# Input loads in another order, retention pair sums on VectorE, and output-projection operands ahead of their gates

## The chip, the cores and the metric

The kernel runs on one core of a Trainium2 chip, as one launch. The metric is device time in microseconds (us) of that launch; the median over several executions counts.

The engines are named as the profile names them: PE is TensorE (matrix products and transposes; PEld are its weight loads), DVE is VectorE, ACT is ScalarE, POOL is GpSimd, and SP is SyncE, which here issues most of the transfers. Each engine works through its own list of instructions in order, and semaphores tie the lists together.

## The reference, cut to what matters

A trunk of two layers over 1024 rows of 1024 features. Each layer scales and shifts its input by vectors made from the conditioning vector `c`, runs a mixer, adds and normalizes, and runs a convolutional feed-forward part.

```python
e = jax.nn.silu(c @ cond_w + cond_b)
for i in range(DEPTH):                       # layer 0: gated_deltanet, layer 1: retention
    mod = (e @ ada_w[i] + ada_b[i])[:, None, :]
    sh1, sc1, g1, sh2, sc2, g2 = jnp.split(mod, 6, axis=-1)
    y = mixers[i % N_MIXERS](x * (1.0 + sc1) + sh1)
    x = layer_norm(DN_ALPHA * x + (1.0 + g1) * y, ln_g[i, 0], ln_b[i, 0])
    y = conv_ffn(x * (1.0 + sc2) + sh2, ...)
    x = layer_norm(DN_ALPHA * x + (1.0 + g2) * y, ln_g[i, 1], ln_b[i, 1])

# retention (4 heads, 8 chunks of 128 rows), its scan and its end
o = einsum(q_n, state) * xi ;  state = state * gamma_c + einsum(k_n * zeta, v_n)
o = intra + inter
o = _standardize(o, 1e-6)                    # per row and head
return (o * silu(gate)) @ w_out
```

## The kernel before

Rows are held transposed for the matrix products. Products are done in three passes: an operand is split into a high part (made by ACT, L89) and the rest (made by DVE, L90), and high x low, low x high and high x high are summed in a PSUM tile (`acc`, `sc` and `mm` are the three kinds of tile). The text is written roughly in order of the work, and a scheduler of the build then decides from it how each engine's list stands; so an edit at one place can also swap neighbours elsewhere.

**The start.** The 1024 rows are two halves of 512, and `x` is loaded half by half and by columns: `load_x(half, c)` issues four transfers for columns `c`. `mod_loads(g)` loads the weight columns of group g (two feature tiles) for the scale `sc1` and shift `sh1`; `mod_cols(g)` multiplies them by `e` on DVE (eight instructions, L500 and L502), sums over partitions by eight small matrix products on PE (L507, result in an `mm` tile), and adds the biases on DVE (L509, L514). `turn` transposes `x` on PE (L521) into an `mm` tile, and `hold` copies transposed tiles aside by ACT (L532), so that they wait for their scale. `first_k(half, f)` scales feature tile f (ACT, L538), splits it and runs the first projections' products on it: into `acc` tiles for half 0, into `sc` tiles for half 1 (L110 to L112). Beside this, steps of later layers' modulation (`bg_ada`, L221 and L223 on DVE) run in the background; each loads two 128x512 tiles (L213) and frees their places when DVE has read them.

**The retention core.** `core(h)` runs eight chunk steps n of head h. `ret_back(h, n, po)` ends each: row statistics on DVE (L1818 to L1821), one power on POOL (L1822, `mv`), the standardized row `on` (DVE, L1824), and after a pause (`yield RL["b"]`) the load of its gate rows, four transposes, and the product with the gate (`ot`, DVE, L1833). The output projection uses a Strassen scheme of seven products over blocks 11, 12, 21, 22 of its operands, and so needs sums of blocks. For n < 4 the blocks 11 and 12 are stored in DRAM (`od`). For n > 3 those of the same columns are loaded again (`op`, L1851), block 22 is stored by ACT's queue (L1852), and four pair sums S1, S2, S4, S3 are made by POOL (L1855), in place, each stored by SP (L1856). The fourth, S3, overwrites the tile from which block 22 is stored. While the core runs, PE also works on the projections of the values (`ret_v`) and on the first products of the output projection.

**The output projection** (`proj_gen`, with `gate` in retention): step n of 56 is one of seven products and one of eight operand blocks j; `ops(n)` loads and splits its two operands (`ab`, `bb`). `ops_ahead(n)` does this a step before it is used. In retention, products 0 and 1 wait with `gate(j)` until head j//2 has stored its blocks (event `("ob", h)`).

Of the kernel before, what the change touches and what calls it, by code (L numbers as in the profile page):

```python
# [15 lines left out]
P = 128  # L16
# [3 lines left out]
HALF = 512  # L20
# [6 lines left out]
ABLK = ("11", "12", "22", "S1", "S2", "S3", "S4")  # L27
# [6 lines left out]
def trunk_kernel(ctx: ExitStack, tc, A):  # L34
    nc = tc.nc
    pe, act, dve, pool, sp = nc.tensor, nc.scalar, nc.vector, nc.gpsimd, nc.sync
# [9 lines left out]
    def tl(tag, shape, dt=F32, name=None):  # L46
        return sb.tile(shape, dt, tag=tag, name=name or tag, bufs=BUFS[tag])
# [13 lines left out]
    def mm_tile():  # L61
        return ps.tile([P, HALF], F32, tag="mm", name="mm", bufs=2)

    def sc_tile():
        return ps.tile([P, HALF], F32, tag="sc", name="sc", bufs=2)
# [16 lines left out]
    def hs(half):  # L82
        return slice(half * HALF, (half + 1) * HALF)
# [71 lines left out]
    def by_cols(banks, w, v, k):  # L155
        for j, bank in enumerate(banks):
            pe.matmul(bank[:, 0:1], w[:, j * P:(j + 1) * P], v[:, k:k + 1], start=(k == 0), stop=(k == KT - 1))
# [33 lines left out]
    def bias_cols(i, j):  # L191
        return ada_b[:, i * 48 + j * 8:i * 48 + j * 8 + 8]
# [294 lines left out]
    def mod_loads(g):  # L487
        w = mw[g] = [tl("hTb" if g < 2 else "qkv", [P, HALF] if g > 1 else [P, 2, HALF], name="mvw") for _ in range(4 if g < 2 else 8)]
        for j, t in enumerate(w):
            sp.dma_start(t, A["ada0"][g][:, 2 * j:2 * j + 2] if g < 2 else A["ada0"][g][:, j])  # L490

    def mod_cols(g):
        w = mw[g]
        n = 2 * P if g == 0 else HALF
        a = tl("t2", [P, HALF], name="mva")[:, 0:n]
        bank = [sc_tile(), sc_tile()] if g == 0 else None
        for k in range(KT):
            wk = w[k // 2][:, k % 2] if g < 2 else w[k]
            if k == 0:
                dve.tensor_scalar(a, wk[:, 0:n], e[:, 0:1], None, ALU.mult)  # L500
            else:
                dve.scalar_tensor_tensor(a, wk[:, 0:n], e[:, k:k + 1], a, ALU.mult, ALU.add)  # L502
            if g == 0:
                by_cols(bank, wk[:, n:], e, k)
        pt = mm_tile()
        for j in range(n // P):
            pe.matmul(pt[:, j:j + 1], a[:, j * P:(j + 1) * P], ones[:, 0:1], start=True, stop=True)  # L507
        c = slice(2 * g, 2 * g + 2)
        dve.scalar_tensor_tensor(sc1[:, c], pt[:, 0:2], 1.0, bias_cols(0, 1)[:, c], ALU.add, ALU.add)  # L509
        if g == 0:  # L510
            for j in range(2):
                dve.tensor_add(sh1[:, j:j + 1], bank[j][:, 0:1], bias_cols(0, 0)[:, j:j + 1])
        else:
            dve.tensor_add(sh1[:, c], pt[:, 2:4], bias_cols(0, 0)[:, c])  # L514
# [3 lines left out]
    def turn(half, f):  # L518
        pt = mm_tile()
        for t in range(4):  # L520
            pe.transpose(pt[:, t * P:(t + 1) * P], xt[half][t][f // 4][:, f % 4 * P:(f % 4 + 1) * P], ident)  # L521
        return pt

    def hold(half, fs):
        for f in fs:
            if half == 0 and f > 3:
                if f % 2 == 0:
                    xT["w"] = tl("wr", [P, 2, HALF], name="xT")
                t = xT["w"][:, f % 2]
            else:  # L530
                t = tl("auh" if half else "xT", [P, HALF], name="xT")
            act.activation(t, turn(half, f), AF.Copy)  # L532
            xT[half, f] = t

    def first_k(half, f):
        src = xT[half, f] if (half, f) in xT else turn(half, f)
        tmp = tl("t2", [P, HALF])
        act.activation(tmp, src, AF.Identity, bias=sh1[:, f:f + 1], scale=sc1[:, f:f + 1])  # L538
        ht = two(("hTa", "hTb")[half], F32R, "hT")
        split(ht[0], ht[1], tmp)  # L540
        hT[half].append(ht)
        if accs[half] is None:
            accs[half] = [sc_tile(), sc_tile()] if half else acc4()
        for n, acc in enumerate(accs[half]):
            mm3(acc, ws[n], f, ht, f == 0, f == KT - 1)
# [4 lines left out]
    def load_x(half, c):  # L550
        for t in range(4):
            if half:
                xt[1][t][c] = tl("auh", [P, HALF], name="xt")
            r0 = half * HALF + t * P
            sp.dma_start(xt[half][t][c], xin[r0:r0 + P, hs(c)])
# [12 lines left out]
    mod_cols(1)  # L568
    hold(0, range(4, 8))
    mod_loads(2)  # L570
    load_x(1, 0)
    first_k(0, 2)
    first_k(0, 3)
    mod_cols(2)
    hold(1, range(4))
    mod_loads(3)
    load_x(1, 1)
    first_k(0, 4)
    first_k(0, 5)
    mod_cols(3)  # L580
    for f in range(4):
        first_k(1, f)
    first_k(0, 6)
# [35 lines left out]
    events = {}  # L619
# [18 lines left out]
    def emit(name, lat=0.0):  # L638
        events[name] = clk[0] + lat
# [635 lines left out]
    def proj_gen(nj, ablk, wsrc, slots, xsrc, G, final, ln_next, tag, ltags, dst, key, mm=pe.matmul, gate=None, gain=None):  # L1275
# [48 lines left out]
        def ops(n):  # L1324
            if n in ready:
                return ready.pop(n)
            p, j = n // nj, n % nj
            an, bn = prods[p][:2]
            early = not gate and p < (7 if final else 5)
            ra, rb = ablk(an, j), bblk(bn, j)  # L1330
            last = an == "22"
            at = ltags[0] if last and j >= nj - ltags[3] else ("wl", "hTb", "wr")[n % 3] if early else ("wl", "wr")[n % 2]
            wt = (ltags[1] if last and j >= nj - ltags[2] else ("wh", "hTb", "hTb")[n % 3] if early
                  else ("wh", "auh")[n % 2] if gate and p > 1 else "wh")
            a = two(at, F32R, "ab")
            split(a[0], a[1], ra)
            w = two(wt, F32R, "bb")
            split(w[0], w[1], rb)
            if bn == "22":
                dve.tensor_tensor(X[j], rb, X[j], ALU.subtract)  # L1340
            with after("a"):
                for st in steps[n + ahead:n + ahead + 1]:
                    load_b(*st)
            return a, w

        def ops_ahead(n):
            if n < len(steps) and not (gate and n <= 2 * nj):
                ready[n] = ops(n)

        xts = [[], []]  # L1350
# [108 lines left out]
        steps = [(bn, j) for _, bn, _ in prods for j in range(nj)]  # L1459
# [4 lines left out]
        for p, (an, bn, fin) in enumerate(prods):  # L1464
# [8 lines left out]
            for j in range(nj):  # L1473
# [4 lines left out]
                a, w = ops(p * nj + j)  # L1478
# [178 lines left out]
    od = dr.tile([8, 7, P, HALF], F32, tag="od", name="od")  # L1657
# [58 lines left out]
    for t in range(4):  # L1716
        if t % 2 == 0:
            xw = tl("lane", [P, 2, HALF], name="xlo")
        x = xw[:, t % 2]
# [96 lines left out]
    def ret_back(h, n, po):  # L1816
        st = tl("st", [P, 2, 6], name="rst")
        dve.bn_stats(st[:, 0], po)  # L1818
        mv = tl("s8", [P, 4], name="mv")
        dve.bn_aggr(mv[:, 0:2], st[:, 0])  # L1820
        dve.tensor_scalar(mv[:, 2:3], mv[:, 1:2], 1e-6, None, ALU.add)  # L1821
        pool.tensor_tensor(mv[:, 3:4], mv[:, 2:3], mhalf[:, 0:1], ALU.pow)  # L1822
        on = tl("t2", [P, HALF], name="on")
        dve.tensor_scalar(on, po, mv[:, 0:1], mv[:, 3:4], ALU.subtract, ALU.mult)  # L1824
        yield RL["b"]
        sl = slice(n * P, (n + 1) * P)
        g = tl("cv", [P, 516], name="gt")[:, 0:HALF]
        sp.dma_start(v4(g), gd[4 * h:4 * h + 4, :, sl].rearrange("j p t -> p j t"))
        pt = mm_tile()
        for j in range(4):  # L1830
            ptr(pt[:, j * P:(j + 1) * P], on[:, j * P:(j + 1) * P])
        ot = tl("cv", [P, 516], name="ot")[:, 0:HALF]
        dve.tensor_mul(ot, pt, g)  # L1833
        s4 = slice(n % 4 * P, (n % 4 + 1) * P)

        def pair_view(t):
            return t.rearrange("p (j a f) -> p a j f", a=2, f=P)

        def blk(nm):
            return od[2 * h:2 * h + 2, ABLK.index(nm), :, s4].rearrange("j p t -> p j t")  # L1840

        ov = pair_view(ot)
        if n < 4:
            for a, nm in enumerate(("11", "12")):
                anchor["x", 1] = act.dma_start(blk(nm), ov[:, a])
            if n == 3:
                emit(("ob", h), RL["o"])
            return
        pv = pair_view(tl("cv", [P, 516], name="op")[:, 0:HALF])
        for a, nm in enumerate(("11", "12")):  # L1850
            sp.dma_start(pv[:, a], blk(nm))  # L1851
        act.dma_start(blk("22"), ov[:, 1])  # L1852
        for d, x, y, op, nm in ((ov[:, 0], ov[:, 0], ov[:, 1], ALU.add, "S1"), (pv[:, 0], ov[:, 0], pv[:, 0], ALU.subtract, "S2"),
                                (pv[:, 1], pv[:, 1], pv[:, 0], ALU.subtract, "S4"), (ov[:, 1], ov[:, 1], pv[:, 0], ALU.subtract, "S3")):
            pool.tensor_tensor(d, x, y, op)  # L1855
            sp.dma_start(blk(nm), d)  # L1856

    def load_qk(h, j):
# [134 lines left out]
```

## Time and profile before

| | us |
|---|---|
| median of 3 runs | 2937.2 (2934.97 to 2941.72) |
| the profiled execution's own time | 2931.49 |
| its span in the trace | 2929.3 |
| busy in the span: PE | 2808.1 (96%) |
| DVE | 2198.4 (75%) |
| ACT | 1316.2 (45%) |
| POOL | 421.1 (14%) |
| retention core and first products of its output projection (1780 to 2140): PE busy | 346.83 of 360.00 |

Times within a trace count from the start of the span. A row of the timeline gives the start, the duration, the engine, the line, the operation with its output and inputs, and in brackets how long the engine was idle before it and what released it. A row of the waits gives an instruction, what it waited for, the total, the number of times and the longest. The mean granted clock of PE was 0.989 of full speed in this execution.

### The profile page before, as it was taken

To read this page: it belongs to the slowest core of one execution; us is meant where nothing else is said; L and a number is where in the kernel's file an instruction comes from. 1 tells how busy PE (TensorE), PEld (TensorE's weight loads), DVE (VectorE), ACT (ScalarE), POOL (GpSimd) and SP (SyncE) were. 2 spreads that over 40 slices of the span, in tenths; PEclk is the share of its full clock that TensorE was granted. 3 is DMA by queue.
4 is the path that set the end of the run, shared out by engine and by line. 5 is a ranking of instruction groups with operands and counts; after the bars stand their busy time and mean duration, and the time that the engine had idled before them with its cause. 6 is when DMAs were issued, how large, how long until landed. Compare 5 with 4: busy or idle time off the path is not lost. (4 is left out here: it accounts for less than half of the span.)

```text
span 2929.3 us, 38823 instructions
## 1 busy us (share of the span) xinstructions
PE 2808.1 (96%) x13638; PEld 2296.3 (78%) x13638; DVE 2198.4 (75%) x3965; ACT 1316.2 (45%) x2457; POOL 421.1 (14%) x485
## 2 busy tenths in 40 slices
PE   8998999999999999999999999999999899999997
PEld 7777877887778888887787877777778688888786
DVE  6695687556788888897687766666697887778888
ACT  3755465443544444536443332221345544444443
POOL 0311220134011111100000000223201011111001
PEclk9999999999999999999999999999999999999999
DMA  8122221354344444863434454555564233335753
GB/s 309 64 80 80 98 91 44 105 187 148 108 150 159 163 157 147 316 218 123 157 110 173 149 181 149 165 172 163 189 235 155 94 137 108 108 108 202 262 158 119
DMA packets 239234, 442.35 MB, mean 151 GB/s; under 512 B 22848, under 2 KB 76352, under 8 KB 239040
## 3 DMA queue, kind: packets, MB, share of 16 engines
q1 hardware_dynamic: 206832, 387.96, 39.4%
q10 hardware_dynamic: 29760, 43.00, 4.0%
q0 software_dynamic: 2448, 8.91, 0.8%
q8 instruction: 107, 1.75, 0.2%
q14 instruction: 87, 0.71, 0.1%
HBM read 331.26 MB, written 108.53 MB: 150 GB/s over the span
## 5 line engine op out<-in xcount | busy, mean ns | idle before, releaser
L1466 PE MATMUL acc<-bb,ab 128*128 128x512 f32 x1800 | 427.5, 393 | 6.5 <-DVE pa L1441 2.5
L1466 PEld LDWEIGHTS acc<-bb,ab 128*128 128x128 f32 x1800 | 338.0, 189 | 81.4 <-DVE bb L90 3.8
L630 PE MATMUL acc<-hT,wh 128*128 128x512 f32 x960 | 300.3, 394 | 0.0
L1605 POOL TENSOR_TENSOR o<-o 128x512 f32<-128x512 f32 x88 | 121.1, 1387 | 810.6 <-DVE o L1598 680.4
L89 ACT ACTIVATE ab<-ar 128x512 fp32r<-128x512 f32 x210 | 129.0, 624 | 184.2 <-PE acc L1466 93.3
L1159 PE MATMUL acc<-T,wb 128*128 128x512 f32 x840 | 204.2, 392 | 7.2 <-DVE wb L90 7.2
L630 PEld LDWEIGHTS acc<-hT,wh 128*128 128x128 f32 x960 | 183.0, 191 | 34.0
L630 PE MATMUL acc<-hT,wl 128*128 128x512 f32 x480 | 202.8, 422 | 0.8 <-DVE qkv L993 0.5
L1159 PEld LDWEIGHTS acc<-T,wb 128*128 128x128 f32 x840 | 157.9, 189 | 43.7 <-DVE wb L90 11.1
L90 DVE TENSOR_TENSOR ab<-ar,ab 128x512 fp32r<-128x512 f32 x210 | 146.4, 703 | 44.2 <-ACT ab L89 44.2
L90 DVE TENSOR_TENSOR wb<-mm,wb 128x512 fp32r<-128x512 f32 x216 | 145.2, 684 | 23.4 <-ACT wb L89 21.7
L90 DVE TENSOR_TENSOR wb<-wr,wb 128x512 fp32r<-128x512 f32 x162 | 111.3, 688 | 65.7 <-ACT wb L89 63.8
L1225 ACT ACTIVATE pc<-acc 128x512 f32<-128x512 f32 x143 | 84.7, 592 | 160.5 <-PE acc L1159 91.6
L89 ACT ACTIVATE wh<-wr 128x1024 fp32r<-128x1024 f32 x101 | 107.0, 1061 | 110.2 <-PE acc L630 50.3
L89 ACT ACTIVATE wb<-mm 128x512 fp32r<-128x512 f32 x216 | 122.3, 593 | 72.8 <-DVE mm L1205 72.1
L90 DVE TENSOR_TENSOR wl<-wr,wh 128x1024 fp32r<-128x1024 f32 x85 | 105.5, 1241 | 61.2 <-ACT wh L89 59.1
L89 ACT ACTIVATE wb<-wr 128x512 fp32r<-128x512 f32 x162 | 99.7, 627 | 96.5 <-DMA wr<-in_ffn_up 53.0
L449 DVE SCALAR_TENSOR_TENSOR qkv<-raw,vc,qkv 128x512 f32<-128x512 f32 x144 | 112.3, 783 | 34.8 <-ACT qkv L447 30.7
L630 PE MATMUL acc<-wh,hT 128*128 128x512 f32 x384 | 135.5, 415 | 0.7 <-DVE vv L90 0.7
L1584 DVE SCALAR_TENSOR_TENSOR o<-g,vc,o 128x512 f32<-128x512 f32 (+2 forms) x176 | 135.2, 786 | 0.7
L223 DVE SCALAR_TENSOR_TENSOR ada<-mvw,e,ada 128x512 f32<-128x512 f32 x140 | 105.9, 757 | 27.0 <-DMA mvw<-in_ada_w 26.5
L110 PE MATMUL acc<-T,wb 128*128 128x512 f32 x292 | 116.6, 399 | 9.9 <-DVE wb L90 9.4
(626 smaller groups left out, 6876.5 us busy)
## 6 DMA issues: line engine op xcount, KB each, us to landing
wr<-in_ffn_up SPq DMA_DIRECT2D x96, 512.0 KB, 4.3
ad<-o SPq DMA_DIRECT2D x154, 256.0 KB, 2.2
ar<-ad SPq DMA_DIRECT2D x154, 256.0 KB, 4.2
mvw<-in_ada_w SPq DMA_DIRECT2D x48, 512.0 KB, 5.5
Br<-in_ffn_down SPq DMA_DIRECT2D x66, 256.0 KB, 3.3
mvw<-in_ada_w SPq DMA_DIRECT2D x64, 256.0 KB, 3.0
wr<-in_ret_wv SPq DMA_DIRECT2D x32, 512.0 KB, 4.2
ar<-od SPq DMA_DIRECT2D x56, 256.0 KB, 5.0
```

Of the source, the lines that this page charges most:

```text
L89: act.activation(dst_h, src, AF.Copy)
L90: eng.tensor_tensor(dst_l, src, dst_h, ALU.subtract)
L110: mm(acc, wl[:, k], hl[0], start=first, stop=False)
L223: dve.scalar_tensor_tensor(a, wr[kk], e[:, k:k + 1], a, ALU.mult, ALU.add)
L449: dve.scalar_tensor_tensor(oh, raw[:, 3 - j:515 - j], w[:, 3 - j:4 - j], oh, ALU.mult, ALU.add)
L630: pq(pe.matmul(out, lhsT, rhs, start=start, stop=stop, **kw), cost)
L1159: return pe.matmul(*a, skip_group_check=True, **kw)
L1225: act.activation(t, X, AF.Copy)
L1466: mm_ = (lambda *a, p=p, onto=onto, **kw: (mm if p < 2 else pe.matmul)(*a, skip_group_check=onto, **kw))
L1584: dve.scalar_tensor_tensor(tv, gv[:, c0 - j:c1 - j], w[:, 2 - j:3 - j], tv, ALU.mult, ALU.add)
L1605: pool.tensor_tensor(o[d], o[x], o[y], op)
```

## The change

It has three parts. At the start, the loads of group 3's weight columns (`mod_loads(3)`) stand right behind those of group 2, ahead of the load of half 1's first columns, and `hold(1, range(4))` and the load of half 1's second columns (`load_x(1, 1)`) stand behind `mod_cols(3)`. In the output projection, the operands of a step are made a step ahead in products 0 and 1 too, if the block's event has been emitted, and always from step 16 on. In the retention core the reload of blocks 11 and 12 is issued ahead of the pause, and the four pair sums are VectorE's.

```diff
@@ -568,16 +568,16 @@
     mod_loads(2)
+    mod_loads(3)
     load_x(1, 0)
     first_k(0, 2)
     first_k(0, 3)
     mod_cols(2)
-    hold(1, range(4))
-    mod_loads(3)
-    load_x(1, 1)
     first_k(0, 4)
     first_k(0, 5)
     mod_cols(3)
+    hold(1, range(4))
+    load_x(1, 1)
     for f in range(4):
         first_k(1, f)
@@ -1344,7 +1344,9 @@
         def ops_ahead(n):
-            if n < len(steps) and not (gate and n <= 2 * nj):
+            if gate and n < 2 * nj and ("ob", n % nj // 2) not in events:
+                return
+            if n < len(steps):
                 ready[n] = ops(n)
@@ -1822,6 +1824,18 @@
         dve.tensor_scalar(on, po, mv[:, 0:1], mv[:, 3:4], ALU.subtract, ALU.mult)
...
+        if n > 3:
+            pv = pair_view(tl("cv", [P, 516], name="op")[:, 0:HALF])
+            for a, nm in enumerate(("11", "12")):
+                sp.dma_start(pv[:, a], blk(nm))
         yield RL["b"]
@@ -1846,13 +1852,10 @@
-        pv = pair_view(tl("cv", [P, 516], name="op")[:, 0:HALF])
-        for a, nm in enumerate(("11", "12")):
-            sp.dma_start(pv[:, a], blk(nm))
         act.dma_start(blk("22"), ov[:, 1])
         for d, x, y, op, nm in (...):
-            pool.tensor_tensor(d, x, y, op)
+            dve.tensor_tensor(d, x, y, op)
             sp.dma_start(blk(nm), d)
```

The numbers of instructions stay the same but for the sums: DVE has 64 more, POOL 64 fewer. Lines behind the new code shift: `on` is L1826 afterwards, the sums are L1858.

PE's list at the start, from the last products that group 2 allows to the small matrix products of group 3 (L507): before, transposes and products of half 1 (`sc`) stand on both sides of it.

```order
L112 MATMUL sc<-hT,wh 128x512
L110 MATMUL sc<-hT,wl 128x512 x2
L507 MATMUL mm<-ones,mva 128x1 x4
L521 MATMUL mm<-cst,xt 128x128 x4
L111 MATMUL sc<-hT,wh 128x512
L112 MATMUL sc<-hT,wh 128x512
L111 MATMUL sc<-hT,wh 128x512
```

The same place of the list afterwards:

```order
L111 MATMUL acc<-hT,wh 128x512
L112 MATMUL acc<-hT,wh 128x512
L507 MATMUL mm<-ones,mva 128x1 x4
L521 MATMUL mm<-cst,xt 128x128 x18
L110 MATMUL sc<-hT,wl 128x512 x2
L521 MATMUL mm<-cst,xt 128x128 x2
L111 MATMUL sc<-hT,wh 128x512
```

All products of half 1 now stand behind the small products of group 3 and behind 18 transposes; 16 of these are `hold(1, range(4))`, and the last two read columns that `load_x(1, 1)` brings.

SP's list of transfers at the same place, before (L490 is `mod_loads`, L555 `load_x`, L213 the background step):

```order
L490 DMA mvw<-in_ada 128x512 x8
L555 DMA xt<-in_x 128x512 x4
L490 DMA mvw<-in_ada 128x512 x8
L213 DMA mvw<-in_ada_w 128x512 x2
L102 DMA wr<-in_gdn_wqkv 128x1024
L213 DMA mvw<-in_ada_w 128x512 x2
L555 DMA xt<-in_x 128x512 x4
L213 DMA mvw<-in_ada_w 128x512 x6
```

And afterwards:

```order
L490 DMA mvw<-in_ada 128x512 x16
L555 DMA xt<-in_x 128x512 x4
L213 DMA mvw<-in_ada_w 128x512 x2
L102 DMA wr<-in_gdn_wqkv 128x1024
L213 DMA mvw<-in_ada_w 128x512 x8
L555 DMA xt<-in_x 128x512 x4
```

The second `L555 x4` is `load_x(1, 1)`; ten background loads stand ahead of it now, and four did. On DVE, the end of group 3 (the last L502, then L509 and L514) among the background steps, before:

```order
L502 SCALAR_TENSOR_TENSOR mva<-mvw,e,mva 128x512
L223 SCALAR_TENSOR_TENSOR ada<-mvw,e,ada 128x512
L90 TENSOR_TENSOR hT<-t_563,hT 128x512
L223 SCALAR_TENSOR_TENSOR ada<-mvw,e,ada 128x512
L90 TENSOR_TENSOR hT<-t_574,hT 128x512
L223 SCALAR_TENSOR_TENSOR ada<-mvw,e,ada 128x512
L509 SCALAR_TENSOR_TENSOR v_172<-mm,vc 128x2
L514 TENSOR_TENSOR v_173<-mm,vc 128x2
L223 SCALAR_TENSOR_TENSOR ada<-mvw,e,ada 128x512
```

And afterwards:

```order
L502 SCALAR_TENSOR_TENSOR mva<-mvw,e,mva 128x512
L223 SCALAR_TENSOR_TENSOR ada<-mvw,e,ada 128x512
L502 SCALAR_TENSOR_TENSOR mva<-mvw,e,mva 128x512
L223 SCALAR_TENSOR_TENSOR ada<-mvw,e,ada 128x512 x2
L509 SCALAR_TENSOR_TENSOR v_172<-mm,vc 128x2
L514 TENSOR_TENSOR v_173<-mm,vc 128x2
L223 SCALAR_TENSOR_TENSOR ada<-mvw,e,ada 128x512
```

One more background step moved ahead of the last L502; two still stand between it and L509, one behind L514. In the retention core, DVE's list at step n = 5 of a head, before, from the mask product `sT` to the split of the next values (`vv`):

```order
L1763 TENSOR_TENSOR sT<-mm,dx 128x128
L1833 TENSOR_TENSOR ot<-mm,gt 128x512
L90 TENSOR_TENSOR sThl<-sT,sThl 128x128
L1818 BN_STATS rst<-sc 128x6
L1820 BN_AGGR mv<-rst 128x2
L1821 TENSOR_SCALAR mv<-mv 128x1
L1824 TENSOR_SCALAR on<-sc,mv 128x512
L90 TENSOR_TENSOR vv<-acc,vv 128x512 x2
```

And afterwards:

```order
L1765 TENSOR_TENSOR sT<-mm,dx 128x128
L1847 TENSOR_TENSOR ot<-mm,gt 128x512
L90 TENSOR_TENSOR sThl<-sT,sThl 128x128
L1858 TENSOR_TENSOR ot<-ot 128x2x128
L1858 TENSOR_TENSOR op<-ot,op 128x2x128
L1858 TENSOR_TENSOR op<-op 128x2x128
L1820 BN_STATS rst<-sc 128x6
L1822 BN_AGGR mv<-rst 128x2
L1823 TENSOR_SCALAR mv<-mv 128x1
L1826 TENSOR_SCALAR on<-sc,mv 128x512
L1858 TENSOR_TENSOR ot<-ot,op 128x2x128
L90 TENSOR_TENSOR vv<-acc,vv 128x512 x2
```

S1, S2 and S4 stand ahead of the statistics, and S3 (`ot<-ot,op`) between `on` and the split of the values. On DVE at the end of product 1 of the output projection (`c` is its four results) and the start of product 2, before:

```order
L90 TENSOR_TENSOR bb<-Br,bb 128x512 x2
L1425 TENSOR_TENSOR c<-acc,rowb 128x512 x4
L1313 TENSOR_TENSOR Br<-Bw 128x512 x2
L90 TENSOR_TENSOR bb<-Br,bb 128x512
L1313 TENSOR_TENSOR Br<-Bw 128x512
L90 TENSOR_TENSOR ab<-ar,ab 128x512
```

And afterwards:

```order
L90 TENSOR_TENSOR bb<-Br,bb 128x512
L1427 TENSOR_TENSOR c<-acc,rowb 128x512 x4
L90 TENSOR_TENSOR bb<-Br,bb 128x512
L1313 TENSOR_TENSOR Br<-Bw 128x512 x2
L90 TENSOR_TENSOR ab<-ar,ab 128x512
```

The operand `ab` of step 16 stands one instruction nearer to the four results, still behind them.

More of the change, by code (lines that the diff above doesn't have):

```diff
@@ L1824, in ret_back, with blk, pair_view @@
         dve.tensor_scalar(on, po, mv[:, 0:1], mv[:, 3:4], ALU.subtract, ALU.mult)
+        s4 = slice(n % 4 * P, (n % 4 + 1) * P)
+        def blk(nm):
+            return od[2 * h:2 * h + 2, ABLK.index(nm), :, s4].rearrange("j p t -> p j t")
+        def pair_view(t):
+            return t.rearrange("p (j a f) -> p a j f", a=2, f=P)
+        if n > 3:
+            pv = pair_view(tl("cv", [P, 516], name="op")[:, 0:HALF])
+            for a, nm in enumerate(("11", "12")):
+                sp.dma_start(pv[:, a], blk(nm))
         yield RL["b"]
@@ L1833, in ret_back @@
         dve.tensor_mul(ot, pt, g)
[L1834 to L1840, printed above, removed]
         ov = pair_view(ot)
```

## The prediction

> **What bounds the kernel now.** I read the page first: how much of the span each engine works.
>
> ```profile
> span 2929.3 us, 38823 instructions
> PE 2808.1 (96%) x13638; PEld 2296.3 (78%) x13638; DVE 2198.4 (75%) x3965; ACT 1316.2 (45%) x2457; POOL 421.1 (14%) x485
> ```
>
> PE is idle for 121.2 us in all (2929.3 - 2808.1). The change does not alter PE's products, so it can only move that idle time and the clock at which PE runs. I therefore read, in each of the three places, what PE waits for, and walk the new lists with durations of the old rows. At the start the view of PE in order of time shows this:
>
> ```profile
> 53.74 1.18 PE L521 MATMUL mm<-cst,xt 128*128 128x128 f32 x8
> 56.29 1.97 PE L521 MATMUL mm<-cst,xt 128*128 128x128 f32 x8 [1.37 <-ACT xT L532]
> 57.91 1.94 PE L110 MATMUL acc<-hT,wl 128*128 128x512 f32 x4
> ...
> 64.27 0.62 PE L110 MATMUL sc<-hT,wl 128*128 128x512 f32 x2
> ...
> 67.44 0.95 PE L507 MATMUL mm<-ones,mva 128*128 128x1 f32 x8
> 68.25 0.64 PE L521 MATMUL mm<-cst,xt 128*128 128x128 f32 x4
> ...
> 84.17 0.73 PE L110 MATMUL sc<-hT,wl 128*128 128x512 f32 x2 [1.09 <-ACT hT L89]
> 86.00 0.50 PE L111 MATMUL sc<-hT,wh 128*128 128x512 f32 x1 [1.09 <-DVE hT L90]
> ...
> 87.42 1.12 PE L633 MATMUL mm<-cst,ab 128*128 128x128 f32 x4
> ```
>
> Between 57.91 and 67.44 PE never waits: behind the 24 products of half 0 (to 64.27) it has products of half 1 to do while DVE makes group 3's columns. The clock in the same stretch (columns: window, its length, PE busy, granted clock):
>
> ```profile
> 54.00:56.30 2.30, 0.93 (x9) 0.97 0.03 7
> 56.30:58.00 1.70, 1.70 (x9) 0.50 0.74 154
> 58.00:60.00 2.00, 2.00 (x8) 0.60 0.97 349
> 60.00:64.00 4.00, 4.00 (x19) 1.00 0.94 340
> 84.00:88.00 4.00, 2.65 (x9) 0.86 0.00 0
> 88.00:92.00 4.00, 4.00 (x15) 0.71 0.18 55
> ```
>
> After an idle stretch of 1.4 us PE ran at half clock for some 3.3 us, a loss of about 1.7 us; the two stalls at 84 and 86 were followed by a loss of 4 x 0.14 + 4 x 0.29 = 1.7 us too.
>
> **The start, step by step.** Rows of ACT, DVE and SP's queue in order of time (the last row is of the page: transfers of this size, and the median time to landing):
>
> ```profile
> 54.23 1.52 ACT L538 ACTIVATE t<-xT,v,v 128x512 f32<-128x512 f32 x2 [5.48 <-DVE v L514]
> ...
> 60.80 10.31 SPq L213 DMA_DIRECT2D mvw<-in_ada_w  x6
> ...
> 64.23 0.74 DVE L502 SCALAR_TENSOR_TENSOR mva<-mvw,e,mva 128x512 f32<-128x512 f32 x1
> 64.98 0.75 DVE L223 SCALAR_TENSOR_TENSOR ada<-mvw,e,ada 128x512 f32<-128x512 f32 x1
> ...
> 68.63 0.75 DVE L223 SCALAR_TENSOR_TENSOR ada<-mvw,e,ada 128x512 f32<-128x512 f32 x1 [1.04 <-DMA mvw<-in_ada_w]
> ...
> mvw<-in_ada_w SPq DMA_DIRECT2D x64, 256.0 KB, 3.0
> ```
>
> 1. Without the 16 transposes of `hold(1, ...)`, PE goes from group 2's small products (done 53.7) to half 0's products. These need ACT's scaling (done 55.75 for both tiles) and a split, 0.6: 56.3. Idle 2.6, of which 1.37 were there before.
> 2. The 24 products, at half clock to about 59.7 and then at 0.23 us each as in the rows 57.91 to 64.27: done about 63.4.
> 3. Then L507 of group 3. Its last input is the last L502, which ended at 64.97. Two splits moved from ahead of it to behind (1.3), but a background step moved ahead, whose operand, issued at 60.80, lands 2.8 later at best (63.6); 63.65 + 0.67 + 0.74 is 65.1 again. PE idle 63.4 to 65.1: 1.7. The small products take 0.8, four transposes 0.5: 66.4.
> 4. The next transposes need the tile that L509 and L514 release. These stand behind two background steps (L223). The second's load can be issued when the step ahead has freed its place. In the rows above, from the end of L223 at 65.73 to the next use of its place at 68.63 are 2.9 us. Before the last L502 the freeing step now ends at about 64.4; + 2.9 = 67.3, + 0.75 + 0.15: 68.2. PE idle 1.8.
> 5. Twelve transposes at 0.11 to 0.15: 69.9. The 17th reads `load_x(1, 1)`. On SP this stands behind ten background loads, the last of which needs the place that the step behind L514 frees, at about 69.8. With the median 3.0 to landing: 73.2. PE idle 3.3.
> 6. From there PE has its products without a wait up to the end of the stretch, where the last tile's scaling and split leave about 1.5 (before: 1.09 + 1.09).
>
> Idle afterwards 2.6 + 1.7 + 1.8 + 3.3 + 1.5 = 10.9; before, 1.37 + 1.09 + 1.09 = 3.6. That is 7.3 more. The clock goes down once more (behind 63 to 73, up to 1.7) and may stay up at 84 to 92 (1.7): I take zero. **Term +7, from +4 to +9**: the low end with landings 1 us sooner in steps 4 and 5 and no new half-clock stretch, the high end with that stretch. I let all of it reach the end: PE's share of the span is 96%, and no idle stretch near the start is long enough to take it up.
>
> [...]
>
> **The pair sums.** The waits of PE, and one of DVE's, from 1780 to 2140 (total, times, longest):
>
> ```profile
> PE sc L1466 <- DVE ab L90: 4.1, 1, 4.1
> PE sc L630 <- DVE on L1824: 4.0, 4, 1.8
> PE acc L630 <- DVE ab L90: 2.8, 1, 2.8
> PE mm L633 <- DVE on L1824: 1.5, 3, 1.2
> PE sc L630 <- DVE Sr L1798: 0.6, 1, 0.6
> PE acc L630 <- DVE bb L90: 0.2, 1, 0.2
> ...
> DVE on L1824 <- POOL mv L1822: 28.1, 24, 3.4
> ```
>
> PE waits 13.2 us in 360. 6.1 of these (`on`, `Sr`) hang on the retention steps, and DVE's `on` waits 28.1 us for the power on POOL, which often stands behind pair sums. So at best 6.1 go. What the 64 sums cost on DVE has no row of their form; the nearest, with DVE's share:
>
> ```profile
> L1763 DVE TENSOR_TENSOR sT<-mm,dx 128x128 f32<-128x128 f32 x32 | 9.0, 281 | 0.0
> L1761 DVE SCALAR_TENSOR_TENSOR kz<-mm,vc,kz 128x256 fp32r<-128x256 f32 x28 | 13.4, 478 | 13.5 <-ACT kz L1760 13.5
> 1780.00:2140.00 360.00, 229.76 (x426) 1.00 0.55 174
> ```
>
> Between 281 (128x128) and 478 (128x256, another operation) I take 0.42 us: 64 x 0.42 = 27 us (18 to 31). DVE has 130 us free there, which covers them, and most stand where DVE waited for POOL. Without that cover they would all be late for `on`, and 27 us would be on the path of the steps.
>
> The new wait is another one. S3 overwrites the tile from which ACT's queue stores block 22, and must wait for that store; on POOL this held up POOL alone:
>
> ```profile
> 1845.84 0.39 ACTq L1852 DMA_DIRECT2D od<-ot  x1
> 1850.76 0.81 DVE L1824 TENSOR_SCALAR on<-sc,mv 128x512 f32<-128x512 f32 x1 [2.35 <-POOL mv L1822]
> 1853.23 0.73 POOL L1855 TENSOR_TENSOR ot<-ot,op 128x256 f32<-128x256 f32 x1 [2.51 <-DMA od<-ot]
> ...
> 1857.15 0.63 PE L633 MATMUL mm<-cst,on 128*128 128x128 f32 x4 [0.17 <-DVE on L1824]
> ```
>
> These are rows of ACT's queue, DVE, POOL and PE. The store took 7.4 us (1845.84 to 1853.23). On DVE, S3 stands at step 5 behind `on` and ahead of two splits of values (0.64 each) and the next statistics. DVE would stand until 1853.2 with these queued; the two splits that were done by 1852.8 come after, and the next `on`, for which PE already waited at 1857.15, is about 1.4 us later. Steps 4 are alike with S3 ahead of the statistics. With 8 steps 4 and 5 in four heads at up to 0.8 on average, the upper end is +6; the lower is -6.1. Most of the other stores land well inside the pause, and only some of `on`'s waits are behind a sum: **term +1, from -6 to +6**, the middle with the one place that I can place on its upper side.
>
> [...]
>
> The earlier reload (SP) moves two issues, about 0.4 us each, ahead of the gate rows' load; SP is not waited for there, so I cost it at nothing; its cover is the pause, and without it `ot` would be 0.9 us later.
>
> **Operands ahead.** The view of time, DVE, at the 4.1 us wait:
>
> ```profile
> 2130.39 1.28 DVE L1313 TENSOR_TENSOR Br<-Bw 128x512 f32<-128x512 f32 x2
> 2131.85 0.69 DVE L90 TENSOR_TENSOR bb<-Br,bb 128x512 fp32r<-128x512 f32 x1 [0.17 <-ACT bb L89]
> 2132.46 0.68 DVE L1313 TENSOR_TENSOR Br<-Bw 128x512 f32<-128x512 f32 x1
> 2133.06 0.69 DVE L90 TENSOR_TENSOR ab<-ar,ab 128x512 fp32r<-128x512 f32 x1
> ```
>
> Behind product 1's results (2130.4) `ab` of step 16 was the fifth instruction and is now the fourth: `bb`, two `Br`, `ab`, each 0.60 to 0.69 behind the one ahead, end at about 2133.0, against 2133.7. **Term -0.7, from -4 to 0**; all 4.1 would go only if it stood ahead of the results, which it does not. The 2.8 us wait is step 0's, which isn't made ahead.
>
> **Sum.** +7 + 1 - 0.7 = +7.3 on the profiled 2931.5, so 2938.8. That execution lies 5.7 us below the median of the three runs; against the median 2937.2 the forecast is 2944.5. 0.2% is 5.9 us, about what a measurement of this kernel tells from no change.
>
> **Rivals.**
> - *The start does not open.* If L507 of group 3 can run by 63.4 because its columns are done 1.7 us sooner, L514 and the background steps move up with it, and `load_x(1, 1)` lands under half 1's first products. For it: group 3's loads are issued earlier. Against: at 64.23 its DVE step waited for nothing that is a load of its own. Start 0: +0.3, 2937.5, the same. Chance 0.17.
> - *Faster: DVE is freed of POOL.* Place: 1857 to 2134. If `on` comes 28.1/24 = 1.2 us sooner in nearly each step, DVE is ahead everywhere, and all of PE's 13.2 us of waits there go: 7 - 13.2 = -6.2, 2931. It decides as soon as the core gives back over 12.9 (7 + 5.9). Against: 6.9 of the 13.2 are operand waits behind PE's own results. Chance 0.12.
> - *Slower still: the store blocks DVE.* With stores of 7 us in most steps 4 and 5: core +6, sum +12.3, 2949.5. For it: 7.4 us in the row above, with 174 GB/s moved beside it. Against: on POOL the wait was 2.5 us. Chance 0.13.
> - *No net change:* the swaps that the scheduler makes elsewhere (each under 1 us) and the ends of the ranges cancel. 2937 to 2940. Chance 0.05.
>
> **How the numbers follow.** The forecast itself has 0.53, its own range +3 to +11 (2940 to 2948). Slower by over 0.2% (above 2943.1): 0.43 of the forecast, all of the blocked store, nothing else: 0.56. The same: 0.10 of the forecast, 0.14 of the unopened start, 0.04 of the faster case, 0.05 of the last: 0.33. Faster: 0.08 of its case and 0.03 of the unopened start: 0.11. The range 2930 to 2951 holds the faster case's price and the blocked store's, and leaves out 0.2.
>
> **What would show it.** In the changed profile: PE idle before L507 of group 3, before its transposes, and before the 17th, in sum near 6.8, and the L633 row near 94.5 where 87.42 stood; DVE's wait of `on` for POOL down from 28.1 to below 10, and in its place waits of L1858 for `od<-ot` of some 10 us in all; sums near 0.42 us; PE's wait at 2133.80 near 3.4. The prediction is wrong if L633 stands before 90, or if PE's waits for `on` vanish without new ones.

## The result and the profile after

| | before | after |
|---|---|---|
| median of 8 runs, us | 2938.4 (2934.1 to 2941.7) | 2945.5 (2942.0 to 2948.1) |
| ratio | | 1.0022 (95%: 1.0013 to 1.0032), +6.5 us |
| span of the profiled execution | 2929.3 | 2944.2 |

The change makes the kernel slower by 0.22%. The two profiled executions lie 14.9 us apart, more than the medians do: that of before lies 7 us below its median, that of after at its own. The page of after begins:

```profile
span 2944.2 us, 38789 instructions
PE 2817.0 (96%) x13638; PEld 2300.2 (78%) x13638; DVE 2220.9 (75%) x4029; ACT 1315.8 (45%) x2457; POOL 372.9 (13%) x421
```

PE's idle time went from 121.2 to 127.2 us. Its busy time rose by 8.9 us although it runs the same 13638 products: the mean granted clock is 0.986 here and was 0.989. Both parts must be followed. Counted by the number of the PE instruction, the 14.9 us split into 9.9 up to the 600th, 2.3 on to the 8800th (the retention core's first step), -1.4 to the 10280th (the start of product 2), 4.6 to the 13200th (in the last product) and -0.4 to the end. Of the 4.6 us, 2.8 are idle time of PE; no run here takes that stretch apart. PE in order of time at the start, after:

```profile
52.47 0.95 PE L507 MATMUL mm<-ones,mva 128*128 128x1 f32 x8
55.87 2.07 PE L110 MATMUL acc<-hT,wl 128*128 128x512 f32 x4 [2.45 <-ACT hT L89]
...
65.30 1.26 PE L507 MATMUL mm<-ones,mva 128*128 128x1 f32 x8 [2.20 <-DVE mva L502]
66.42 1.09 PE L521 MATMUL mm<-cst,xt 128*128 128x128 f32 x4
68.40 2.89 PE L521 MATMUL mm<-cst,xt 128*128 128x128 f32 x12 [0.89 <-DVE v L514]
74.16 0.66 PE L521 MATMUL mm<-cst,xt 128*128 128x128 f32 x2 [2.86 <-DMA xt<-in_x]
76.15 0.69 PE L521 MATMUL mm<-cst,xt 128*128 128x128 f32 x2 [0.48 <-DMA xt<-in_x]
...
95.75 0.51 PE L111 MATMUL sc<-hT,wh 128*128 128x512 f32 x1 [0.71 <-DVE hT L90]
97.18 0.66 PE L633 MATMUL mm<-cst,ab 128*128 128x128 f32 x4 [0.22 <-ACT ab L595]
```

The brackets sum to 9.8 us; before, those of this stretch came to 3.7 (1.37, 0.16, 1.09, 1.09). L633 stands 9.8 us later than the 87.42 of before; counted from the small products of group 2 (52.47 here, 52.93 before) it is 10.2. The clock (window, length, PE busy, granted clock):

```profile
64.00:68.00 4.00, 2.21 (x12) 0.74 0.45 149
68.00:72.00 4.00, 2.89 (x12) 0.50 0.50 154
72.00:78.00 6.00, 3.37 (x10) 0.50 0.54 175
78.00:84.00 6.00, 6.00 (x27) 0.87 0.25 89
...
88.00:92.00 4.00, 4.00 (x19) 1.00 0.00 0
```

PE stands idle for 28% to 45% of each of the first three windows, and from about 66 on it runs at half clock, and on for 1.6 us when the work is back. Busy time x (1 - clock) in these four rows is 4.5 us; the half clock of before at 84 to 92 (1.5) is gone. The retention core and the projection, waits of PE and DVE from 1780 to 2155 (total, times, longest):

```profile
PE sc L630 <- DVE on L1826: 3.7, 2, 1.9
PE acc L630 <- DVE ab L90: 2.8, 1, 2.8
PE acc L630 <- DVE vv L90: 1.3, 3, 0.6
PE sc L1468 <- DVE ab L90: 0.9, 1, 0.9
...
DVE on L1826 <- POOL mv L1824: 15.1, 23, 0.7
DVE ot L1858 <- DMA od<-ot: 13.4, 11, 3.5
...
DVE ot L1847 <- DMA od<-op: 6.2, 5, 2.8
```

DVE's wait for the power fell from 28.1 to 15.1 us. In its place came a wait of its sums for stores (13.4), and one that the prediction did not have: the product with the gate (`ot`, now L1847) waits 6.2 us for the stores of sums that lie in `op` tiles. PE waits for `on` 3.9 us in all, where it waited 5.5. The wait of 4.1 us at the start of product 2 is gone; a step later PE waits 0.9 for `ab`.

### The profile page after: what moved, and what is told of

The parts are those of the page before. It is cut to its first block, busy times and chain, and to the rows that moved or that the text cites. A ratio compares the mean times of both kernels' runs of the same rounds, so it can differ in the third digit from the quotient of the medians.

```text
span 2944.2 us, 38789 instructions
## 1 busy us (share of the span) xinstructions
PE 2817.0 (96%) x13638; PEld 2300.2 (78%) x13638; DVE 2220.9 (75%) x4029; ACT 1315.8 (45%) x2457; POOL 372.9 (13%) x421
## 5 line engine op out<-in xcount | busy, mean ns | idle before, releaser
L1468 PE MATMUL acc<-bb,ab 128*128 128x512 f32 x1800 | 426.6, 392 | 6.9 <-DVE pa L1443 2.9
L1468 PEld LDWEIGHTS acc<-bb,ab 128*128 128x128 f32 x1800 | 337.5, 189 | 81.0 <-issue 3.3
L1159 PEld LDWEIGHTS acc<-T,wb 128*128 128x128 f32 x840 | 159.3, 191 | 46.3 <-DVE wb L90 13.4
```

The source lines that it names most:

```text
L1159: return pe.matmul(*a, skip_group_check=True, **kw)
L1468: mm_ = (lambda *a, p=p, onto=onto, **kw: (mm if p < 2 else pe.matmul)(*a, skip_group_check=onto, **kw))
```

## Experiments

The theory: the start carries the loss, the operands ahead give some back, the sums are near nothing. The rival was that the sums, or swaps of neighbours, carry it. All medians are of five rounds, with before on the same chip at 2937.2 to 2938.6.

| kernel | median, us | ratio to before (95%) |
|---|---|---|
| start's part alone | 2951.3 | 1.0047 (1.0033 to 1.0060) |
| only group 3's loads ahead | 2937.0 | 0.9997 (0.9989 to 1.0006) |
| operands ahead alone | 2935.1 | 0.9987 (0.9979 to 0.9996) |
| sums alone | 2941.8 | 1.0010 (1.0001 to 1.0019) |
| all but the start | 2938.5 | 0.9998 (0.9989 to 1.0007) |
| the same, S3 in a tile of its own | 2934.4 | 0.9982 (0.9973 to 0.9991) |
| all but the start, sums on POOL | 2934.6 | 0.9986 (0.9978 to 0.9995) |
| start and operands ahead | 2948.0 | 1.0032 (1.0021 to 1.0043) |
| start, columns in tiles of their own | 2953.5 | 1.0048 (1.0035 to 1.0062) |
| best version with these tiles | 2933.4 | 0.9987 (0.9978 to 0.9997) |
| start's part by half | 2953.5 | 1.0047 (1.0030 to 1.0064) |

**The parts one by one.** Start alone: the start's hunk of the diff on the kernel before.

> The kernel before with the start's part alone. Theory: the start carries more than the whole loss, because all products of half 1 stand behind group 3's columns and behind the load of half 1's second columns, and the other two parts give some of it back. Then this kernel is 8 to 12 us slower than before, slower than the whole change (+7), and the L633 row that stood at 87.42 stands near 97. Rival: PE's idle time at the start is made up by shorter waits later, and the loss is in the core; then it is within 3 us of before.

It came out at +0.47%, some 14 us. PE has the same waits as in the whole change, in other sizes. From the small products of group 2 to L633 it takes 43.1 us here, 44.7 in the whole change and 34.5 before, so most of the loss is made at the start:

```profile
66.34 1.02 PE L507 MATMUL mm<-ones,mva 128*128 128x1 f32 x8 [1.11 <-DVE mva L502]
69.48 2.89 PE L521 MATMUL mm<-cst,xt 128*128 128x128 f32 x12 [1.63 <-DVE v L514]
...
95.75 0.50 PE L111 MATMUL sc<-hT,wh 128*128 128x512 f32 x1 [0.71 <-DVE hT L90]
```

Only the loads ahead:

```diff
     mod_loads(2)
+    mod_loads(3)
     load_x(1, 0)
...
-    mod_loads(3)
     load_x(1, 1)
```

> Only the loads of group 3's columns moved ahead of half 1's first load; PE's list is that of before, word for word. Theory: the cost of the start comes from where the transposes and half 1's second load stand, not from these loads; within 2 us of before, L633 within 1 us of 87.42. Rival: the eight transfers of 256 KB ahead delay half 1's first columns by some 5 us, PE waits for these at 53.7, and it is 3 to 5 us slower.

No difference: the order of these loads is not the cause. What is left of the start's part is that `hold(1, range(4))` and `load_x(1, 1)` stand behind `mod_cols(3)`.

Operands ahead alone: the hunk in `ops_ahead` on the kernel before.

> The kernel before with the operands ahead of their gates alone. Theory: the operands of step 16 are made before product 1's results are taken, so the wait of 4.05 us at 2133.80 goes: 3 to 4 us faster. Rival (the prediction's reading): the operand still stands behind the results and only one instruction nearer; 0.7 us faster, not to be told from no change, with a wait of 3.4 us left in the trace.

It gave -0.13%, 3.8 us. PE passes from product 1 to product 2 (L1468) without the gap of 4.05 us:

```profile
2131.40 4.81 PE L630 MATMUL acc<-bb,ab 128*128 128x512 f32 x20 [0.23 <-DVE bb L90]
2136.25 0.73 PE L1468 MATMUL sc<-bb,ab 128*128 128x512 f32 x2
...
2143.62 0.73 PE L1468 MATMUL sc<-bb,ab 128*128 128x512 f32 x2 [0.93 <-DVE ab L90]
```

Sums alone: the hunks in `ret_back` on the kernel before.

> The kernel before with the pair sums on DVE and the reload ahead of the pause alone. Theory: S3's wait for block 22's store now stops DVE and costs 2 to 4 us in the core, against some 2 us of waits for the power that go: +1 to +3 us, with DVE waits of L1856 for stores of some 10 us and PE waits for DVE's `on` as before. Rival: DVE freed of POOL gains, 3 to 6 us faster.

It gave +0.10%. But the core did not lose it. PE's waits for `on` there were 4.9 us (5.5 before), and the place where this kernel loses is the end of the kernel. There the scheduler's new order puts one `ab` of the last product behind rows of the final normalization. PE's waits from 2800 to the end, first of this kernel, then of before:

```profile
PE acc L630 <- DVE ab L90: 2.1, 1, 2.1
```

```profile
PE acc L630 <- DVE ab L90: 0.7, 1, 0.7
```

From PE's 13200th instruction, in that product, to the end it took 120.6 us, before 118.6. Four of the kernels have that swapped end and take 120.5 to 120.7 us there: this one, the next, and two of the start's runs below. The other nine, the whole change among them, take 117.4 to 118.6. Of the 2.0 us between this kernel and before, 1.4 are the longer wait (2.1 against 0.7); the rest is not taken apart.

**What the sums are worth.** All but the start, then with S3 in a tile of its own, then with the sums back on POOL:

> The whole change without the start's part (the start as before). Theory: the start carries the loss (6 idle us and some 3 of clock), so without it the other two parts leave a gain: the operands ahead give 3.5 back, the sums are worth -1 to +3; together 3935 is out of reach but 2935 to 2938, -0.13% to 0. Rival: the sums or swaps of neighbours carry the loss, and it stays 3 us or more slower than before.

(The 3935 in it is a slip; it should be a figure just below 2935.) No difference from before. It has the swapped end: 120.5 us.

```diff
+        s3 = pair_view(tl("t2", [P, HALF], name="s3"))[:, 0]
         for d, x, y, op, nm in (..., (ov[:, 1], ov[:, 1], pv[:, 0], ALU.subtract, "S3")):
...
-(ov[:, 1], ov[:, 1], pv[:, 0], ALU.subtract, "S3")
+(s3, ov[:, 1], pv[:, 0], ALU.subtract, "S3")
```

> As the run without the start's part, but S3 is written to a tile of its own instead of over the tile from which block 22 is stored, so that it does not wait for that store. Theory: DVE's waits of its sums for stores (19.4 us in the run of the sums alone) fall below 5, and where `on` stood behind such a wait PE's stalls shorten: 1 to 3 us faster than the run without the start's part, 3 to 6 us faster than before. Rival: the waits on DVE fall where nothing hung on them; within 1 us of that run.

This is the fastest version by its ratio, 0.18% faster than before; the intervals of the operands ahead alone and of the next run overlap with its own. DVE's waits for stores from 1780 to 2145, first all but the start, then with the tile of its own:

```profile
DVE ot L1858 <- DMA od<-ot: 19.2, 12, 3.5
```

```profile
DVE ot L1847 <- DMA od<-ot: 2.3, 4, 0.8
```

19.2 us of waiting went from DVE, and PE gained next to nothing there. From its 8800th to its 10280th instruction, PE took 339.9 us with the waits and 339.7 without. The second figure holds a stretch at a lower clock (0.84 granted from 1990 to 2000), so it could hide a gain of up to 1.7 us; but PE's waits for `on` are 6.0 us in both kernels. Of the gain over the run before it (4.1 us by the medians), 2.7 lie at the end of the kernel (117.8 us against 120.5): PE's list there is not swapped. So the rival was right on the core: those waits fall where nothing hangs on them.

```diff
-            dve.tensor_tensor(d, x, y, op)
+            pool.tensor_tensor(d, x, y, op)
```

> As the run without the start's part, but the pair sums stay on POOL (the reload ahead of the pause and the operands ahead remain). Theory: moving the sums is worth about nothing in time since PE's stalls for `on` were 7.4 us before and 6.6 after; within 2 us of the run of the operands ahead alone (-3.5). Rival: the sums on POOL cost the powers' waits, and this one is 3 us slower than the run with the sums on DVE and a tile of its own.

-0.14%, as the operands ahead alone (-0.13%). Moving the sums, and issuing the reload ahead, are worth nothing that can be measured here.

**Do the parts add up?**

> The start's part and the operands ahead, without the sums' part. Theory: the parts add up: +8 to +12 of the start (its run alone measured +12.7) and -3.5: +5 to +9, about where the whole change is (+7). If the start alone is really +12.7, this is +9; if that run lay high, +5.

+0.32%, 9.4 us. With operands ahead worth -3.8, sums at 0, and an end that is swapped in some kernels (2.3), the start's part is worth 13.8 alone, 13.2 from this run, and 6.5 + 0.6 + 2.3 = 9.4 from the whole change against all but the start. Nine of it is seen at the start: PE's first 600 instructions took 150.4 to 152.8 us in the five profiles with the start's part or half of it, and 140.4 to 144.3 in the eight without. The rest lies from there to PE's 8800th instruction, at the start of the retention core (about 145 to 1790 us), where the five took 1649.6 us on average and the eight 1645.7. The idle time there differs by under 1 us, so most of it is PE's busy time on the same products; whether that is chance stays open.

**Which of the start's waits counts?** Half 1's second columns in tiles of their own, so that their load can be early:

```diff
-                xt[1][t][c] = tl("auh", [P, HALF], name="xt")
+                xt[1][t][c] = tl("cv", [P, 516], name="xt")[:, 0:HALF] if c else tl("auh", [P, HALF], name="xt")
```

> The start's part alone, but half 1's second columns get four tiles of their own (the `cv` kind), so that their load needs no place freed by the transposes and stands ahead of the background loads. Theory: the start's loss (about +9 to +10) is the sum of waits in a row: for the last L502, for L514, and for these columns. The last (2.86 + 0.48 idle, and part of the half clock) goes: +4 to +7, with the 17th transpose not waiting for a transfer. Rival: whatever comes last, half 1's products start no earlier (DVE's background steps or the scaling then end the wait), and it stays at +9 or more.

The wait for the transfer is gone, and nothing is gained that the medians can tell: +0.48%, some 15 us. This kernel has the swapped end (120.7), which leaves some 13 for the start, against 13.8 in the start alone. PE in order of time:

```profile
70.41 3.54 PE L521 MATMUL mm<-cst,xt 128*128 128x128 f32 x16 [2.54 <-DVE v L514]
...
94.23 0.97 PE L110 MATMUL sc<-hT,wl 128*128 128x512 f32 x2 [2.92 <-ACT hT L89]
...
97.78 1.12 PE L633 MATMUL mm<-cst,ab 128*128 128x128 f32 x4
```

The 2.92 us at 94.23 took the place of the 2.86 and 0.48: the last tile's high part comes from ACT too late. ACT just before it:

```profile
89.19 0.60 ACT L595 ACTIVATE ab<-acc 128x512 f32<-128x512 f32 x1 [3.22 <-PE mm L521]
...
91.78 0.81 ACT L538 ACTIVATE t<-mm,v,v 128x512 f32<-128x512 f32 x1
...
93.49 0.68 ACT L89 ACTIVATE hT<-t 128x512 fp32r<-128x512 f32 x1
```

The scaling of that tile (L538) stands in ACT's list behind five instructions that copy half 0's results out of `acc`, the first of them at 89.19 after 3.22 us of idle time. So this wait comes from the order of ACT's list, and not from a lack of time on ACT. Much earlier ACT also stands idle, here in the whole change, and in the row below it in this kernel:

```profile
67.55 0.60 ACT L532 ACTIVATE xT<-mm 128x512 f32<-128x512 f32 x1 [11.21 <-PE mm L521]
```

```profile
67.91 0.60 ACT L532 ACTIVATE xT<-mm 128x512 f32<-128x512 f32 x1 [9.21 <-PE mm L521]
```

In these 9 to 11 us, before, it copied, scaled and split half 1's first tiles; from 67 on it has ten scalings (L538) still to do, where six were left before. The rival was right on the time, but not on its reason: half 1's products do start earlier, 18.8 us behind group 2's small products against 21.1 in the start alone, and lose it again at the last tile. The waits in a row are not a sum of separate costs. That work which is given out late ends late by one chain or another fits these rows, but is argued and not shown.

> The best version so far (sums on DVE with a tile of its own for S3, operands ahead, the start as before) with the same four tiles for half 1's second columns. PE's list is the same but for a few rows at the start and for the swaps that the start's part also makes in layer 0's feed-forward part and its output projection. Theory: at the start the wait of 1.66 behind the small products shortens by at most that, and the swaps cost about as much: within 2 us of that version, -3 to -7 against before. Rival: the swaps themselves cost 2 to 3 us (the profiles with them were 2.7 us longer between 150 and 1790 us), and the version loses most of its gain.

-0.13%, not to be told from the version without these tiles (-0.18%). From PE's 600th to its 8800th instruction it took 1645.4 us, with the swaps in layer 0 that the start's part makes as well: they cost nothing here.

The start's part by half: `hold(1, range(2))` ahead of group 3, `hold(1, range(2, 4))` and the load behind it.

> The start's part by half: two of half 1's four tiles are held (transposed and copied) ahead of group 3's columns as before, two and the second columns' load behind them. Theory after the run with tiles of their own: the waits don't add up one by one; what is lost is work of PE and ACT on half 1 (12 us of ACT idle at 56 to 67 in the whole change), which cannot be given out before group 3's small products. With half of that work ahead PE has 12 products for the wait for the last L502, which goes; the waits for L514 and for the columns stay in part: half 1's end (the second row of L633) between the two, 90 to 94.5 where 87.42 and 97.18 stood, and +3 to +6 us, up to 2 us more if the end of the kernel has the swapped order that cost 2.3 us. Rival: the loss hangs on the columns' load alone, which stands as late as in the whole change; then +8 or more.

+0.47%, on the side of the rival. The wait for the last L502 went as expected, but the second columns land as late as in the whole change:

```profile
71.20 0.63 PE L521 MATMUL mm<-cst,xt 128*128 128x128 f32 x4 [1.32 <-DVE v L514]
74.91 0.66 PE L521 MATMUL mm<-cst,xt 128*128 128x128 f32 x2 [3.08 <-DMA xt<-in_x]
```

So giving back half of the early work is not enough; from group 2's small products to L633 it takes 42.3 us. Its first 600 PE instructions took 150.4 us, 1.3 us less than in the whole change and 8 more than without the start's part. It also has a swapped end (120.5).

## Why the prediction was right, and where it was not

The forecast of 2944.5 us met 2945.5. The way and the place of the loss were foreseen, but that the number came so close is in part luck: the start cost more than its term (some 9 us at the start itself, 9.4 to 13.8 by the medians), the operands ahead gave back more than theirs, and the two errors cancel.

- **Start, +7 (+4 to +9): the mechanism held, its clock was mis-sized.** The steps came out closely on DVE and SP (rows of after):

```profile
64.41 0.74 DVE L502 SCALAR_TENSOR_TENSOR mva<-mvw,e,mva 128x512 f32<-128x512 f32 x1
...
67.37 0.75 DVE L223 SCALAR_TENSOR_TENSOR ada<-mvw,e,ada 128x512 f32<-128x512 f32 x1 [1.15 <-DMA mvw<-in_ada_w]
...
68.11 0.15 DVE L514 TENSOR_TENSOR v<-mm,vc 128x2 f32<-128x2 f32 x1
...
70.69 1.75 SPq L555 DMA_DIRECT2D xt<-in_x  x4
```

  L502 ends at 65.15 (forecast 65.1), L514 starts at 68.11 and takes 0.15 (forecast to be done at 68.2), the columns land at 74.1 (73.2). Idle time rose by 6.1 us (7.3). The step that failed is "the clock ... I take zero": the half clock from about 66 to 80 costs 4.5 us and the stretch that goes is worth 1.5. L633 at 97.18 instead of 94.5 is this. The idle stretches of PE there are 0.48 to 2.86 us long, and the granted clock around them is 0.74, 0.50 and 0.50.
- **The 17th transpose's wait as a price of 3.3 us** was wrong as a price: taken away, it came back at ACT. The sum of idle times was a good estimate of the idle time; it is not a list of prices that can be taken away one by one.
- **Sums, +1 (-6 to +6): right.** One sum takes 0.42 us, as taken:

```profile
L1858 DVE TENSOR_TENSOR ot<-ot,op 128x256 f32<-128x256 f32 x16 | 6.8, 424 | 13.5 <-DMA od<-ot 13.4
L1858 DVE TENSOR_TENSOR ot<-ot 128x256 f32<-128x256 f32 x16 | 6.8, 422 | 0.1
```

  S3 does wait on DVE for the store (13.4 us; forecast some 10), and `on` waits less for POOL (15.1, not below 10: the power itself takes 0.55, the median of its 32 rows, and that remains). From its 8800th instruction to the end of product 1, PE took 2.6 us more than before, but two half-clock stretches (0.72 granted from 2000 to 2006 and from 2071 to 2077) cost up to 3.4. Both follow waits that before has too, 1.8 us for `on` and 2.8 for `ab`, and after which before ran on at full clock (1.00 from 1983 to 2040, around the wait that ends at 1988.15, and 1.00 from 2053 to 2063). That the store's wait costs `on` 1.4 us at step 5 is not borne out: freeing DVE of it left PE's waits for `on` at 6.0 us.
- **Operands ahead, -0.7 (-4 to 0): wrong in size, at the bound.** The failing step is "`ab` of step 16 was the fifth instruction and is now the fourth". The rows that I took for step 16 in the new list are step 17's; step 16's stand a step earlier, ahead of the results. What is said of step 16's place above, under the change, is wrong in the same way. DVE after:

```profile
2136.81 0.68 DVE L90 TENSOR_TENSOR ab<-ar,ab 128x512 fp32r<-128x512 f32 x1
2138.92 0.69 DVE L90 TENSOR_TENSOR bb<-Br,bb 128x512 fp32r<-128x512 f32 x1 [1.43 <-ACT bb L89]
2140.43 0.69 DVE L1427 TENSOR_TENSOR c<-acc,rowb 128x512 f32<-128x512 f32 x1 [0.82 <-PE acc L630]
...
2146.94 0.69 DVE L90 TENSOR_TENSOR ab<-ar,ab 128x512 fp32r<-128x512 f32 x1
```

  PE enters product 2 at 2144.53, before the `ab` of 2146.94 exists. In the run of this part alone 3.8 us came back (1.2 to 6.2). In the profiles it is less: from PE's 8800th to its 13200th instruction the seven kernels with this part took 1018.7 us on average and the six without it 1020.9, as smaller waits such as the 0.9 a step later follow.
- **Of the rivals,** the unopened start fell (three waits opened), and the freed DVE too: PE's waits for `on` stayed at 3.9 us, and what the projection gave back came from the operands. The blocked store did not show either: DVE's waits for stores were there (13.4 and 6.2 us), but hardly any of them reached PE.

## What to carry to other kernels

A list of transfers or scalings moved behind a wait can cost more than the one wait that the trace names, since the engines had work to do in that time; taking that wait away shows whether it was a price. In an order of repeated rows, count which step a row belongs to before putting a price on its place. A kernel whose scheduler rebuilds the order can gain or lose 2 us at an end that the edit never touched, so set the last 100 us of the traces against each other before crediting an edit.

## What the runs showed of the hardware

The same wait, 2.8 us for `ab` of step 0, was followed by full clock in one execution and by a half-clock stretch in another. PE around it in steps of 3.4 us (PE's busy time and, third figure after the length, its granted clock), before and after:

```profile
2053.00:2056.40 3.40, 1.92 (x14) 1.00 0.92 302
2056.40:2059.80 3.40, 2.13 (x8) 1.00 0.45 150
```

```profile
2069.60:2073.00 3.40, 1.51 (x6) 1.00 0.28 84
2073.00:2076.40 3.40, 3.40 (x6) 0.50 0.28 77
```

Before, the two rows with the wait are at full clock, and so are the 3.4 us behind them (2059.80 to 2063.20). After, the row behind the wait runs at 0.50, with PE busy all through, which costs 1.7 us; the next 3.4 us are at 1.00 again. What decides between the two is not shown by these rows.

In the profiles of all kernels, PE's idle time from 145 to 1790 us lies within 4 us (60 to 64), while its busy time for the same products spreads over 8 us (1582 to 1590). So most of the spread in that stretch is busy time, not waits. Over the whole span the mean granted clock goes from 0.984 (spans of 2951.7 and 2952.5 us) to 0.990 (2925.8 us). The waits of 1.8 and 2.8 us on PE that both before and after have cost their own length, and behind them nothing in the one and up to 1.7 us each in the other.
